# A two-mixer inference step on one core: gated quarters stored from the load queue one slot later, weights of the second mixer in other memory, and its first features interleaved

## The chip, the cores and the metric

The kernel runs on one core of a Trainium2 chip. The time is the device time of one execution in microseconds (us), which for one core is that core's own. Five engines have instruction queues of their own: TensorE (PE, the matmuls, with PEld for the weight loads that run beside them), VectorE (DVE), ScalarE (ACT), GpSimd (POOL) and SyncE (SP, which here only issues transfers). An instruction that waits holds up everything behind it in its queue.

## The reference

A step of a model with two layers over 1024 prompt rows and 128 sample rows of width 1024 (1152 rows, nine tiles of 128), all in float32. Layer A:

```
proj = xn @ w_in                      # 1024 x 6144: u, v, z of 2048 columns each
u, v = gelu(proj[u, v]);  v = layernorm(v)
s = einsum(causal w_s per group of 256 columns, v) + b_s      # mixes rows in chunks of 128
x = x + (u * s * silu(z)) @ w_out     # 2048 x 1024
```

Layer B is an mLSTM: a projection to 4096 columns, a short causal convolution, block-diagonal q, k and v, gates, a matrix memory of four heads in chunks of 64 rows, and an output projection. The eight running streams bring their memories with them and return them. At the end come a last norm and all new states.

## The kernel before, in words

Every matmul in float32 is done as three products in a faster format: each operand is split into a rounded part (hi, a CAST by ACT) and the remainder (lo, a subtraction by DVE, both at L89 and L90 in `split`), and hi·hi, lo·hi and hi·lo are added up in PSUM. A weight tile is therefore ready only when a load has landed, ACT has cast it and DVE has subtracted.

The program runs in stages, in this order.

1. The v projection of layer A (to about 222 us): a loop over four column blocks c and nine row tiles n (L403 on). In the first column block the row tiles are normalised, transposed on PE and split into `Xh` and `Xl` on the way (`norm`, `enter_a`).
2. The u and z projections with the gating, sixteen features f of 128 columns (about 222 to 658 us, L463 to L567). Per feature there are seven products i = 0 to 6, each for two pairs p of row quarters (288 rows each); a product is 12 matmuls of 288 columns. Seven products give the four quarter results of u and z by adding and subtracting the sums (a scheme like Strassen's), so results stay in PSUM or SBUF between products: product 0 leaves `c1` (L497, a copy by ACT out of the accumulator `al`), product 2 goes on in `al` and gives u of the first quarter after a gelu (L503), product 3 leaves `e5`, products 4 and 5 give the two z quarters (add, tanh, multiply, times `Sg`), product 6 gives the other u quarter `y`. Product 2 of a pair cannot start before the copy `c1` of this pair is done, since it writes over `al`.
   `Sg` is the spatial gate: three loads `vh` of v rows, a normalisation by ACT (L531), matmuls `s_` with the group's weights (L539 to L546). Every second feature, `Group` loads and prepares the next group's weights (`wr`, `bs`, `wT`, `rsb`).
   Gated quarters (`uq`, and `y` in the tile `c1`) are written to memory `o_d` by `rows_of` (L481), whose DMA is issued by ACT. The weights of the next features (`fetch_uz`, `prep_uz`) come over SP's queue; two of the seven combinations are sums built by POOL (L369 to L377).
3. The output projection of layer A (658 to 872 us, L638 on), which reads `o_d` back as `or`, splits it into `os`, and adds the residual in `half_out`.
4. Layer B's features (872 to about 1150 us, L811 on), three row blocks b for each feature: the `Feature` class, with `inputs`, then `values` and `keys` one and two steps later. Its first weights are loaded by `w_first` (L664).
5. Gates, decode streams, memory chunks, the output and the last norm (to 1992 us).

PE's instructions are kept in the program's order (class `Ordered`). The order of the other engines and of the queues is set when the program is built, by a scheduler that estimates durations; a tile pool says how many buffers a name has, and where a pool is closed and another opened in its place, the new tiles wait for the last readers of the old ones.

Of the kernel before, what the change touches and what calls it, by code (L numbers as in the profile page):

```python
# [15 lines left out]
P = 128  # L16
# [54 lines left out]
def trunk_kernel(ctx: ExitStack, tc: tile.TileContext, ins: dict, outs: list):  # L71
# [116 lines left out]
    QT = 288  # L188
    KH = KD // 2
    Xh = xp.tile([P, KD, NT * P], F32R, name="Xh")  # L190
    Xl = xp.tile([P, KD, NT * P], F32R, name="Xl")

    S1, S2, S4 = ([xp.tile([P, 2, KH, QT], F32R, name=f"{nm}_{p}") for p in range(2)] for nm in ("S1", "S2", "S4"))
    aw = X_stack.enter_context(tc.tile_pool(name="aw", bufs=1))
# [91 lines left out]
    class Group:  # L286
# [12 lines left out]
        def transposed(self):  # L299
            wT = self.wT = aw.tile([P, 2, P], F32, name="wT")  # L300
            tp = ps.tile([P, P], F32, name="sm")
            T.transpose(tp, self.wr, ident)
            V.tensor_copy(out=wT[:, 0], in_=tp)
            self.w16 = aw.tile([SL, SB, SL], F32, name="w16")
            V.tensor_copy(out=self.w16, in_=wT[:SL, 0, :SL].unsqueeze(1).to_broadcast([SL, SB, SL]))
# [6 lines left out]
        def sums(self):  # L312
            rs = ps.tile([P, 2, P], F32, name="sm")
            T.matmul(rs[:, 0], ones, self.wT[:, 0], start=True, stop=True)
            T.matmul(rs[:, 1], ones, self.wT[:, 1], start=True, stop=True)
            self.rsb = aw.tile([P, 2, P], F32, name="rsb")
            V.tensor_copy(out=self.rsb, in_=rs)
# [64 lines left out]
    for c in range(4):  # L382
        if c:
            wv = [split_b(fetch_b(a_w[:, k, E + c * DH:E + (c + 1) * DH])) for k in range(KD)]
        for n in range(NT):
# [25 lines left out]
            pv = ps.tile([P, DH], F32, name="sm")  # L411
            for k in range(KD):
                mm3(pv, Xh[:, k, ns], Xl[:, k, ns], wv[k][:, 0], wv[k][:, 1], k == 0, k == KD - 1)
            if c == 0 and n == 0:
                enter_a(1)
                xs_[2] = norm(2, V)
                x_[3] = load_x(3)
            vt = vp.tile([P, DH], F32, name="v")
# [41 lines left out]
    def both(s):  # L460
        return s[:, 0], s[:, 1]

    for f in range(NF):  # L463
        g, i2 = divmod(f, 2)
# [16 lines left out]
        def rows_of(o, q):  # L481
            A.dma_start(out=o_d[f * P:(f + 1) * P, quarter(q)], in_=o)

        for i in range(7):
            for p in range(2):
                q0, q1 = 2 * p, 2 * p + 1
# [14 lines left out]
                elif i == 2:  # L501
                    uq[p] = az.tile([P, QT], F32, name="uq", bufs=3)
                    A.activation(out=uq[p], in_=acc, func=AF.Gelu_apprx_tanh)  # L503
                elif i == 3:
                    e5[p] = az.tile([P, QT], F32, name="e5")
                    A.copy(out=e5[p], in_=acc)
                    G.tensor_tensor(out=e5[p], in0=e5[p], in1=c1[p], op=ALU.add)
                elif i in (4, 5):
                    z, q = (e5[p], q1) if i == 4 else (U2[p], q0)
                    V.tensor_tensor(out=z, in0=acc, in1=z, op=ALU.add)  # L510
                    t = az.tile([P, QT], F32, name="t", bufs=3)
                    A.activation(out=t, in_=z, func=AF.Tanh, scale=0.5)
                    V.scalar_tensor_tensor(out=t, in0=t, scalar=1.0, in1=z, op0=ALU.add, op1=ALU.mult)
                    G.tensor_tensor(out=t, in0=t, in1=Sg[:, quarter(q)], op=ALU.mult)
                    if i == 4:
                        tz[p] = t
                    else:
                        V.scalar_tensor_tensor(out=uq[p], in0=uq[p], scalar=0.5, in1=t, op0=ALU.mult, op1=ALU.mult)
                        rows_of(uq[p], q0)
                else:  # L520
                    y = c1[p]
                    V.tensor_tensor(out=y, in0=acc, in1=y, op=ALU.add)
                    A.activation(out=y, in_=y, func=AF.Gelu_apprx_tanh)
                    V.scalar_tensor_tensor(out=y, in0=y, scalar=0.5, in1=tz[p], op0=ALU.mult, op1=ALU.mult)
                    rows_of(y, q1)
            if i < 3:

# [4 lines left out]
                if b == 2:  # L532
# [5 lines left out]
                    S.dma_start(out=sgu_v[0].rearrange("b t e -> (b t) e")[:, f * P:(f + 1) * P], in_=gv[:, 2])  # L538
            if 0 < i < 4:  # L539
                b = i - 1  # L540
                s_ = ps.tile([P, 3, P], F32, name="sm")
# [5 lines left out]
            if i2 == 1 and g + 1 < 8:  # L547
                if i == 3:
                    grp = Group(g + 1)
                elif i > 3:  # L550
                    (grp.transposed, grp.sample, grp.sums)[i - 4]()
            if f + 1 < NF:
# [3 lines left out]
            else:  # L556
# [8 lines left out]
                if i == 6:  # L565
                    split_wo(0, 9)
    X_stack.close()  # L567

# [3 lines left out]
    xs_stack = ExitStack()  # L572
    kp_ = xs_stack.enter_context(tc.tile_pool(name="kp", bufs=1, side="right"))
    ow_stack = ExitStack()
    w2 = ow_stack.enter_context(tc.tile_pool(name="w2", bufs=7))
    ow = ow_stack.enter_context(tc.tile_pool(name="ow", bufs=5))
    xh = [xtp.tile([P, KD, BT], F32R, name="xh") for _ in range(NB)]
# [27 lines left out]

    xa = ow.tile([P, NT, DH], F32, name="xa", bufs=1)
    xs_ = {}

    def half_out(n, c, po):

        cs = slice(c * DH, (c + 1) * DH)
        xv = xa[:, n] if c == 0 else ow.tile([P, DH], F32, name="xb", bufs=3)
        S.dma_start(out=xv, in_=rows(n, ins["x_prompt"], ins["x_sample"])[:, cs])
# [16 lines left out]
    for c in range(2):  # L630
        for b in range(NB):
            po = [ps.tile([P, DH], F32, name="sm") for _ in range(3)]
            for f in range(NF):
# [20 lines left out]
                if c == 1 and b and f in (4, 8, 12):  # L654
                    enter(3 * b - 4 + f // 4)
            for j in range(3):
                half_out(3 * b + j, c, po[j])
    ow_stack.close()
    A_stack.close()
    wp = ctx.enter_context(tc.tile_pool(name="wp", bufs=6))  # L660
    rawp = ctx.enter_context(tc.tile_pool(name="rawp", bufs=4))


    w_first = load_w(b_w[:, :, 0:P])  # L664
    bw_stack = ExitStack()
# [27 lines left out]
    class Feature:  # L693
# [31 lines left out]
        def inputs(self, b):  # L725
# [7 lines left out]
            if b == 2:  # L733
                A.copy(out=xms[:, :, 3:], in_=pm[:, 256:].rearrange("p (b j) -> p b j", b=SB))
                self.xsc = bw.tile([P, P], F32, name="xsc")
                A.copy(out=self.xsc, in_=pm[:, 256:])
            xc = self.xc[b] = bw.tile([P, BT], F32, name="xc", bufs=4)
            parts = [(xc[:, :npr], [xmp[:, b * BT + t:b * BT + t + npr] for t in range(4)])]
# [72 lines left out]
    done = {}  # L811
    feats = [Feature(0)]
    for t in range(3 * NF):
        f, b = divmod(t, NB)
        ft = feats[f]
        ft.inputs(b)
        if b == 0:
            ft.gate_weights()
        if f == 0 and b < 2:
            for n in ((6,), (7, 8))[b]:  # L820
                enter(n)
        if t:
            feats[(t - 1) // NB].values((t - 1) % NB)
        if t > 1:
            feats[(t - 2) // NB].keys((t - 2) % NB)
        if b == 1:
            ft.history()
            if f + 1 < NF:
                feats.append(Feature(f + 1))
            else:  # L830
                z_weights(0)
# [743 lines left out]
```

## Time and profile before

| | |
|---|---|
| runs shown | 1994.90, 2000.48, 2000.66 us; median 2000.48 us |
| profiled execution | 1994.11 us, of it 1992.4 us span from the first to the last instruction |
| mean granted TensorE clock | 0.985 of full speed |
| busy: PE, PEld | 1910.1 us (96%), 1690.7 us (85%) |
| busy: DVE, ACT, POOL | 1261.9 us (63%), 848.2 us (43%), 652.4 us (33%) |
| memory | 203.07 MB read, 123.02 MB written, 164 GB/s over the span |

In the profile a row of a timeline gives a start, a duration, the engine, the line in the kernel, what is written and read, and in brackets how long the engine had been idle before and what ended that. `ACTq` and `SPq` are the instructions with which ACT and SP issue transfers. Idle time is worth most on PE, since PE is busy 96% of the time; the other engines' idle time counts only where PE waits for them.

### The profile page before, as it was taken

How to read it: one execution, taken by the hardware profiler on the slowest of the kernel's cores; microseconds unless marked ns; L12 is line 12 of the kernel's file. 1: busy time of each engine (PE TensorE's matmuls, PEld its weight loads, DVE VectorE, ACT ScalarE, POOL GpSimd, SP SyncE). 2: the span in 40 equal slices, each digit the busy share in tenths (PEclk: the TensorE clock that was granted, in tenths of full speed). 3: DMA queues.
4: the chain of work that ended last, by engine and by line, in shares of the span. 5: the costliest groups of instructions: out<-in, count | busy, mean ns of one | idle time of the engine just before them, and what ended most of it. 6: DMA issues, size and time to landing. Idle time of an engine off the chain costs nothing.

```text
span 1992.4 us, 32048 instructions
## 1 busy us (share of the span) xinstructions
PE 1910.1 (96%) x11553; PEld 1690.7 (85%) x11553; DVE 1261.9 (63%) x2490; ACT 848.2 (43%) x1729; POOL 652.4 (33%) x669
## 2 busy tenths in 40 slices
PE   7999999999999899989999999999999999999998
PEld 5888898999999778869999989888977778778887
DVE  4732466666666454556676665222398799799897
ACT  5422444444444333445555554321254344344454
POOL 2000245444444000014444421100045345436466
PEclk9999999999999999999999999999999999999999
DMA  6222332233333745415555564777898788786433
GB/s 210 85 95 76 106 89 84 86 98 100 97 92 103 228 151 155 152 57 143 161 154 164 163 181 141 212 227 251 256 314 271 243 282 258 242 261 200 152 122 127
DMA packets 345692, 328.22 MB, mean 165 GB/s; under 512 B 28165, under 2 KB 276949, under 8 KB 345533
## 3 DMA queue, kind: packets, MB, share of 16 engines
q1 hardware_dynamic: 279596, 251.59, 41.6%
q10 hardware_dynamic: 65936, 74.58, 11.8%
q8 instruction: 91, 1.49, 0.3%
q14 instruction: 69, 0.56, 0.1%
HBM read 203.07 MB, written 123.02 MB: 164 GB/s over the span
## 4 chain that ended last, share of the span: by engine, by line
PE 45%; DVE 12%; DMA 9%; ACT 2%; issue 2%; POOL 1%; SPq 1%; ACTq 0%; POOLq 0%; DVEq 0%
PE sm L58 45%; DVE Cst L1265 2%; DMA cw<-cw_d 2%; DVE c L1116 2%; DMA raw<-in_b_w_in 1%; DVE Cl L90 1%; DVE qT L1239 1%; DMA out<-c 1%; DMA c<-in_state_mlstm_C 1%; DMA st_d<-w 1%; DVE raw L1348 1%; DVE bst L1305 1%; DMA vv<-vb_d 1%; DVE x L1367 1%; DMA raw<-in_b_w_out 1%
## 5 line engine op out<-in xcount | busy, mean ns | idle before, releaser
L58 PE MATMUL sm<-xh,w 128*128 128x384 f32 x1536 | 414.9, 344 | 8.5 <-issue 6.9
L58 PEld LDWEIGHTS sm<-xh,w 128*128 128x128 f32 x1536 | 285.1, 191 | 17.0 <-issue 13.3
L58 PE MATMUL sm<-xl,w 128*128 128x384 f32 x768 | 262.8, 342 | 1.2 <-DVE xl L90 1.2
L58 PE MATMUL sm<-Xh,w 128*128 128x288 f32 x1024 | 222.5, 302 | 18.8 <-ACT c L497 18.8
L90 DVE TENSOR_TENSOR w<-r,w 128x512 fp32r<-128x512 f32 x176 | 140.3, 806 | 117.3 <-ACT w L89 117.1
L58 PE MATMUL sm<-w,o 128*128 128x512 f32 x864 | 209.8, 398 | 2.6 <-ACT o L89 1.2
L58 PE MATMUL sm<-w,os 128*128 128x512 f32 x864 | 200.2, 393 | 6.7 <-ACT os L89 6.7
L58 PEld LDWEIGHTS sm<-w,os 128*128 128x128 f32 x864 | 162.6, 189 | 42.7 <-ACT os L89 9.2
L58 PEld LDWEIGHTS sm<-w,o 128*128 128x128 f32 x864 | 159.8, 188 | 40.6 <-ACT hn L1317 1.7
L58 PEld LDWEIGHTS sm<-Xh,w 128*128 128x128 f32 x1024 | 169.8, 190 | 22.5 <-ACT c L497 21.5
L58 PE MATMUL sm<-w,Xh 128*128 128x512 f32 x576 | 182.4, 398 | 4.3 <-ACT Xh L89 2.9
L58 PE MATMUL sm<-S,w 128*128 128x288 f32 x1152 | 165.6, 300 | 0.0
L90 DVE TENSOR_TENSOR w<-raw,w 128x1024 fp32r<-128x1024 f32 x44 | 56.8, 1290 | 168.9 <-ACT w L89 164.0
L58 PEld LDWEIGHTS sm<-S,w 128*128 128x128 f32 x1152 | 158.2, 191 | 0.0
L58 PE MATMUL sm<-Xl,w 128*128 128x288 f32 x512 | 152.1, 297 | 0.0
L58 PEld LDWEIGHTS sm<-xl,w 128*128 128x128 f32 x768 | 146.7, 191 | 1.4 <-DVE xl L90 1.4
L89 ACT CAST w<-r 128x512 fp32r<-128x512 f32 x176 | 105.8, 618 | 70.5 <-POOL r L371 34.6
L58 PEld LDWEIGHTS sm<-w,Xh 128*128 128x128 f32 x576 | 109.4, 192 | 28.6 <-ACT Xh L89 3.5
L58 PE MATMUL sm<-w,Xl 128*128 128x512 f32 x288 | 113.7, 395 | 0.0
L89 ACT CAST w<-raw 128x1024 fp32r<-128x1024 f32 (+1 forms) x56 | 55.2, 988 | 129.9 <-DMA raw<-in_b_w_in 105.4
L90 DVE TENSOR_TENSOR os<-or,os 128x384 fp32r<-128x384 f32 x96 | 53.0, 556 | 89.3 <-ACT os L89 89.3
L58 PE MATMUL sm<-va,k 128*128 128x258 f32 (+1 forms) x768 | 103.8, 284 | 4.5 <-ACT ev L1109 1.7
(306 smaller groups left out, 3745.9 us busy)
## 6 DMA issues: line engine op xcount, KB each, us to landing
c<-in_state_mlstm_C SPq DMA_DIRECT2D x64, 512.0 KB
out<-c SPq DMA_DIRECT2D x64, 512.0 KB
r<-in_a_w_in SPq DMA_DIRECT2D x96, 256.0 KB
or<-o_d SPq DMA_DIRECT2D x96, 192.0 KB
raw<-in_b_w_in SPq DMA_DIRECT2D x32, 512.0 KB
qT<-q_d SPq DMA_DIRECT2D x40, 256.0 KB
vh<-v_d SPq DMA_DIRECT2D x48, 192.0 KB
vb_d<-st ACTq DMA_DIRECT2D x48, 192.0 KB
```

What stands on the lines that cost most here:

```text
L58: ins = fn(*args, **kw)
L89: first = A.copy(out=hi, in_=src)
L90: (lo_eng or V).tensor_tensor(out=lo, in0=src, in1=f32(hi), op=ALU.subtract)
L1116: V.scalar_tensor_tensor(out=c0[:, cc], in0=c0[:, cc], scalar=decB[:, d.h, 8 + b:9 + b], in1=pc, op0=ALU.mult, op1=ALU.add)
L1239: V.tensor_tensor(out=u.g["qT"], in0=u.g["qT"], in1=u.g["cw"][:, 1:2].to_broadcast([P, DC, P]), op=ALU.mult)
L1265: V.scalar_tensor_tensor(out=Cst[:, c, a, :w], in0=Cst[:, c, a, :w], scalar=decB[:, h, n:n + 1], in1=pc, op0=ALU.mult, op1=ALU.add)
L1305: V.bn_stats(out=bst[:, a], in_=hn[:, a, :256])
L1348: V.scalar_tensor_tensor(out=og[:, c], in0=u.pT[:, c], scalar=colB[:, HNG, 4 * h + c:4 * h + c + 1], in1=g["sk"][:, c], op0=ALU.mult, op1= ...
L1367: V.tensor_tensor(out=xv, in0=xv, in1=py, op=ALU.add)
```

## The change

Eight things are changed.

- `rows_of` no longer issues a store at once from ACT. It puts it on a list, and the list is issued from SP's queue at the end of the next product slot (the last feature's at the end of the stage).
- Of the two multiplications by `Sg` per pair, that of product 5 moves from POOL to DVE; that of product 4 stays on POOL but is written in the slot of product 5.
- The gate's matmuls `s_` for the three row blocks stand after products 2, 3 and 4 instead of 1, 2 and 3.
- `Group` for the next group starts at product 0 instead of 3, its parts at products 2, 4 and 6 instead of 4, 5 and 6; `wT` and `rsb` have two buffers.
- In the v projection, the second row tile's transposes stand inside the first tile's loop, at k = 5.
- `S1` and `S2` change places in memory, and lie before `Xh` and `Xl`; the output projection's pools are ordered anew, and the row tiles `xa` and `xb` have a pool of their own.
- The pools of layer B's weights are opened, and `w_first` loaded, before the last row block's `half_out`, instead of after all of them.
- Layer B's first two features take turns: (feature, block) = (0,0), (0,1), (1,0), (1,1), (0,2), (1,2), then as before; the last row tiles (6, 7, 8) are transposed during (1,0) and (1,1) instead of (0,0) and (0,1); `xc` has six buffers.

```diff
@@ layer A's features
         def rows_of(o, q):
-            A.dma_start(out=o_d[f * P:(f + 1) * P, quarter(q)], in_=o)
+            late.append(lambda f=f: S.dma_start(out=o_d[f * P:(f + 1) * P, quarter(q)], in_=o))
 
         for i in range(7):
+            rows_out_, late = late, []
...
-                    G.tensor_tensor(out=t, in0=t, in1=Sg[:, quarter(q)], op=ALU.mult)
                     if i == 4:
                         tz[p] = t
                     else:
+                        V.tensor_tensor(out=t, in0=t, in1=Sg[:, quarter(q)], op=ALU.mult)
+                        G.tensor_tensor(out=tz[p], in0=tz[p], in1=Sg[:, quarter(q1)], op=ALU.mult)
...
+            for fn in rows_out_:
+                fn()
...
-            if 0 < i < 4:
-                b = i - 1
+            if 1 < i < 5:
+                b = i - 2
...
-                if i == 3:
-                    grp = Group(g + 1)
-                elif i > 3:
-                    (grp.transposed, grp.sample, grp.sums)[i - 4]()
+                if i == 0:
+                    nxt_grp = Group(g + 1)
+                elif i % 2 == 0:
+                    (nxt_grp.transposed, nxt_grp.sample, nxt_grp.sums)[i // 2 - 1]()
@@ the first row tiles
             for k in range(KD):
+                if c == 0 and n == 0 and k == 5:
+                    enter_a(1)
+                    xs_[2] = norm(2, V)
+                    x_[3] = load_x(3)
                 mm3(pv, Xh[:, k, ns], Xl[:, k, ns], wv[k][:, 0], wv[k][:, 1], k == 0, k == KD - 1)
-            if c == 0 and n == 0:
-                enter_a(1)
-                xs_[2] = norm(2, V)
-                x_[3] = load_x(3)
@@ the end of layer A's output projection
+            if c == 1 and b == 2:
+                ow_stack.close()
+                A_stack.close()
+                rawp = ctx.enter_context(tc.tile_pool(name="rawp", bufs=4))
+                wp = ctx.enter_context(tc.tile_pool(name="wp", bufs=6))
+                w_first = load_w(b_w[:, :, 0:P])
             for j in range(3):
                 half_out(3 * b + j, c, po[j])
-    ow_stack.close()
-    A_stack.close()
-    wp = ctx.enter_context(tc.tile_pool(name="wp", bufs=6))
-    rawp = ctx.enter_context(tc.tile_pool(name="rawp", bufs=4))
-    w_first = load_w(b_w[:, :, 0:P])
@@ layer B's features
-    feats = [Feature(0)]
-    for t in range(3 * NF):
-        f, b = divmod(t, NB)
+    feats = [Feature(0), Feature(1)]
+    steps = [(0, 0), (0, 1), (1, 0), (1, 1), (0, 2), (1, 2)] + [divmod(t, NB) for t in range(2 * NB, NF * NB)]
+    for t, (f, b) in enumerate(steps):
```

How the instructions stand on three queues. First ACT's, at the end of one feature of stage 2 and the start of the next; `c1_3276` and `c1_3291` are the two finished quarters `y` of the feature that ends, `c1_3594` and `c1_3609` the copies that the next feature's product 2 waits for. Before:

```order
L482 DMA o_d_89<-c1_3276 128x288
L523 ACTIVATE c1_3291<-c1_3291 128x288
L497 COPY c1_3594<-sm_3581 128x288
L482 DMA o_d_89<-uq_3356 128x288
L482 DMA o_d_89<-c1_3291 128x288
L497 COPY c1_3609<-sm_3596 128x288
L89 CAST w_3747<-r_3390 128x512
L482 DMA o_d_89<-uq_3370 128x288
```

The same place of the changed kernel (`c1_3274` and `c1_3289` end, `c1_3592` and `c1_3607` are the copies):

```order
L526 ACTIVATE c1_3274<-c1_3274 128x288
L89 CAST w_3699<-r_3527 128x512
L526 ACTIVATE c1_3289<-c1_3289 128x288
L499 COPY c1_3592<-sm_3579 128x288
L499 COPY c1_3607<-sm_3594 128x288
L89 CAST w_3742<-r_3397 128x512
L89 CAST w_3784<-r_3439 128x512
```

The second copy stood behind two stores, and now follows the first one directly.

SP's queue at the same place, where loads of weights `r` and of gate rows `vh` stand (`out_2` is a store of the sample rows' v, `gv` and `wr` are small loads for it and for the next group). Before:

```order
L538 DMA out_2<-gv_3693 128x128
L535 DMA gv_3991<-in_a_ln_g 128x128
L535 DMA gv_3991<-in_a_ln_b 128x128
L291 DMA wr_4045<-in_a_w_s 128x128
L204 DMA r_3708<-in_a_w_in 128x4x128
L204 DMA r_3750<-in_a_w_in 128x4x128
L475 DMA vh_3874<-v_d1_91 128x3x128
L204 DMA r_3789<-in_a_w_in 128x4x128
```

The changed kernel, with the four stores of the feature that ends:

```order
L483 DMA o_d_89<-uq_3357 128x288
L483 DMA o_d_89<-c1_3274 128x288
L483 DMA o_d_89<-c1_3289 128x288
L204 DMA r_3703<-in_a_w_in 128x4x128
L483 DMA o_d_89<-uq_3371 128x288
L204 DMA r_3745<-in_a_w_in 128x4x128
L204 DMA r_3787<-in_a_w_in 128x4x128
L476 DMA vh_3872<-v_d1_91 128x3x128
```

One store stands between the first and the second weight load, the other three ahead of both.

ACT's queue where layer A ends and layer B begins: `xb` are the last row tiles, `w_8426` and `w_8387` the first weight tile of layer B. Before:

```order
L615 DMA x1_d6_125<-xb_8372 128x512
L621 ACTIVATE xs_8376,ss2_8377<-xb_8372 128x512
L615 DMA x1_d7_126<-xb_8386 128x512
L621 ACTIVATE xs_8390,ss2_8391<-xb_8386 128x512
L615 DMA x1_d8_127<-xb_8400 128x512
L621 ACTIVATE xs_8404,ss2_8405<-xb_8400 128x512
L89 CAST w_8426<-raw_8424 128x1024
L89 CAST w_8595<-raw_8593 128x1024
```

The changed kernel:

```order
L626 DMA x1_d6_125<-xb_8390 128x512
L632 ACTIVATE xs_8394,ss2_8395<-xb_8390 128x512
L89 CAST w_8387<-raw_8385 128x1024
L626 DMA x1_d7_126<-xb_8404 128x512
L632 ACTIVATE xs_8408,ss2_8409<-xb_8404 128x512
L89 CAST w_8468<-raw_8466 128x1024
L626 DMA x1_d8_127<-xb_8418 128x512
L632 ACTIVATE xs_8422,ss2_8423<-xb_8418 128x512
```

The first cast moved ahead of two row tiles' work, the second ahead of one's.

## Rows read from the trace of the kernel before

**Rows 1.** The page, busy time of each engine.

```profile
PE   1910.1 (96%) x11553; PEld 1690.7 (85%) x11553; DVE 1261.9 (63%) x2490; ACT 848.2 (43%) x1729; POOL 652.4 (33%) x669
```

**Rows 2.** Waits of PE, whole run: total us, times, longest.

```profile
PE sm L58 <- ACT c L497: 18.8, 11, 2.5
...
PE sm L58 <- DVE w L305: 3.3, 5, 0.9
...
PE sm L58 <- ACT vh L531: 2.5, 1, 2.5
```

**Rows 3.** Busy us by window: PE, PEld, DVE, ACT, POOL, clock, DMA.

```profile
220.00:600.00 380.00, 356.31 (x2613) 350.36 (x2612) 246.55 (x420) 166.25 (x398) 180.09 (x171) 0.98 0.34 97
```

**Rows 4.** Timeline of all engines over one feature's end: start, us, work, idle before.

```profile
466.62 1.27 ACT L531 ACTIVATE vh<-vh,nmr,rstd 128x128 f32<-128x128 f32 x3 [2.15 <-DMA vh<-v_d]
...
469.87 0.23 DVE L296 COPY bs<-bs 128x128 f32<-128x128 f32 x1 [2.75 <-DMA bs<-in_a_b_s]
...
475.49 0.63 ACT L89 CAST w<-r 128x512 fp32r<-128x512 f32 x1 [0.75 <-POOL r L371]
...
477.21 0.38 ACT L497 COPY c<-sm 128x288 f32<-128x288 f32 x1
...
477.39 0.83 PE L58 MATMUL sm<-wT,vh 128*128 128x128 f32 x6
...
478.81 1.38 POOL L377 TENSOR_TENSOR r<-r 128x512 f32<-128x512 f32 x1 [0.68 <-POOL t L514]
478.97 1.53 DVE L518 SCALAR_TENSOR_TENSOR uq<-uq,t 128x288 f32<-128x288 f32 x1
...
481.39 0.45 DVE L518 SCALAR_TENSOR_TENSOR uq<-uq,t 128x288 f32<-128x288 f32 x1
481.50 0.33 ACTq L482 DMA_DIRECT2D o_d<-c  x1
481.87 0.40 ACT L497 COPY c<-sm 128x288 f32<-128x288 f32 x1 [4.28 <-DVE uq L518]
...
482.32 0.40 PE L58 MATMUL sm<-Xh,w 128*128 128x288 f32 x1 [2.52 <-ACT c L497]
...
485.31 4.28 PE L58 MATMUL sm<-S,w 128*128 128x288 f32 x24
```

**Rows 5.** Timeline of PE, one product of a feature without a wait.

```profile
504.01 3.35 PE L58 MATMUL sm<-S,w 128*128 128x288 f32 x24
```

**Rows 6.** Timeline of SP and PE where stage 2 ends and 3 begins.

```profile
658.04 0.33 SPq L198 DMA_DIRECT2D gB<-in_norm_g  x1
658.42 1.37 SPq L645 DMA_DIRECT2D or<-o_d  x3
...
664.69 3.67 PE L58 MATMUL sm<-w,os 128*128 128x512 f32 x8 [6.68 <-ACT os L89]
```

**Rows 7.** Timeline where stage 3 ends and layer B begins.

```profile
871.69 0.38 SPq L144 DMA_DIRECT2D raw<-in_b_w_in  x1
...
874.03 0.75 DVE L627 SCALAR_TENSOR_TENSOR xs<-xb,rr,gB 128x512 f32<-128x512 f32 x1
...
877.36 1.04 ACT L89 CAST w<-raw 128x1024 fp32r<-128x1024 f32 x1 [3.61 <-DMA raw<-in_b_w_in]
...
878.44 1.22 DVE L90 TENSOR_TENSOR w<-raw,w 128x1024 fp32r<-128x1024 f32 x1 [1.34 <-ACT w L89]
...
879.72 1.01 PE L58 MATMUL sm<-xh,w 128*128 128x384 f32 x2 [0.23 <-DVE w L90]
...
894.56 0.44 PE L58 MATMUL sm<-xh,w 128*128 128x384 f32 x1 [1.45 <-ACT xh L89]
896.15 0.45 PE L58 MATMUL sm<-xl,w 128*128 128x384 f32 x1 [1.15 <-DVE xl L90]
```

**Rows 8.** Timeline of PE in the head, between the first two row tiles.

```profile
19.07 1.91 PE L58 MATMUL sm<-ident,xs 128*128 128x128 f32 x16
23.87 1.22 PE L58 MATMUL sm<-w,Xh 128*128 128x512 f32 x2 [2.89 <-ACT Xh L89]
```

More of the change, by code (lines that the diff above doesn't have):

```diff
@@ L189, in trunk_kernel @@
     KH = KD // 2
+    S2, S1, S4 = ([xp.tile([P, 2, KH, QT], F32R, name=f"{nm}_{p}") for p in range(2)] for nm in ("S2", "S1", "S4"))
     Xh = xp.tile([P, KD, NT * P], F32R, name="Xh")
     Xl = xp.tile([P, KD, NT * P], F32R, name="Xl")
-    S1, S2, S4 = ([xp.tile([P, 2, KH, QT], F32R, name=f"{nm}_{p}") for p in range(2)] for nm in ("S1", "S2", "S4"))
     aw = X_stack.enter_context(tc.tile_pool(name="aw", bufs=1))
@@ L299, in transposed @@
         def transposed(self):
-            wT = self.wT = aw.tile([P, 2, P], F32, name="wT")
+            wT = self.wT = aw.tile([P, 2, P], F32, name="wT", bufs=2)
             tp = ps.tile([P, P], F32, name="sm")
@@ L315, in sums @@
             T.matmul(rs[:, 1], ones, self.wT[:, 1], start=True, stop=True)
-            self.rsb = aw.tile([P, 2, P], F32, name="rsb")
+            self.rsb = aw.tile([P, 2, P], F32, name="rsb", bufs=2)
             V.tensor_copy(out=self.rsb, in_=rs)
@@ L461, in both @@
         return s[:, 0], s[:, 1]
+    late = []
     for f in range(NF):
@@ L566, in trunk_kernel @@
                     split_wo(0, 9)
+        if i2 == 1 and g + 1 < 8:
+            grp = nxt_grp
+    for fn in late:
+        fn()
     X_stack.close()
@@ L573, in trunk_kernel @@
     kp_ = xs_stack.enter_context(tc.tile_pool(name="kp", bufs=1, side="right"))
+    xa_stack = ExitStack()
+    xap = xa_stack.enter_context(tc.tile_pool(name="xap", bufs=1, side="right"))
     ow_stack = ExitStack()
+    ow = ow_stack.enter_context(tc.tile_pool(name="ow", bufs=5))
     w2 = ow_stack.enter_context(tc.tile_pool(name="w2", bufs=7))
-    ow = ow_stack.enter_context(tc.tile_pool(name="ow", bufs=5))
     xh = [xtp.tile([P, KD, BT], F32R, name="xh") for _ in range(NB)]
@@ L604, in enter @@
         transpose_x(xs_.pop(n), lambda ks: (xh[b][:, ks, js], xl[b][:, ks, js]))
-    xa = ow.tile([P, NT, DH], F32, name="xa", bufs=1)
+    xa = xap.tile([P, NT, DH], F32, name="xa")
     xs_ = {}
@@ L611, in half_out @@
         cs = slice(c * DH, (c + 1) * DH)
-        xv = xa[:, n] if c == 0 else ow.tile([P, DH], F32, name="xb", bufs=3)
+        xv = xa[:, n] if c == 0 else xap.tile([P, DH], F32, name="xb", bufs=3)
         S.dma_start(out=xv, in_=rows(n, ins["x_prompt"], ins["x_sample"])[:, cs])
@@ L655, in trunk_kernel @@
                     enter(3 * b - 4 + f // 4)
+            if c == 1 and b == 2:
[4 more added lines that the diff above has]
+                w_first = load_w(b_w[:, :, 0:P])
             for j in range(3):
                 half_out(3 * b + j, c, po[j])
-    ow_stack.close()
-    A_stack.close()
-    wp = ctx.enter_context(tc.tile_pool(name="wp", bufs=6))
-    rawp = ctx.enter_context(tc.tile_pool(name="rawp", bufs=4))
-    w_first = load_w(b_w[:, :, 0:P])
+    xa_stack.close()
     bw_stack = ExitStack()
@@ L736, in inputs @@
                 A.copy(out=self.xsc, in_=pm[:, 256:])
-            xc = self.xc[b] = bw.tile([P, BT], F32, name="xc", bufs=4)
+            xc = self.xc[b] = bw.tile([P, BT], F32, name="xc", bufs=6)
             parts = [(xc[:, :npr], [xmp[:, b * BT + t:b * BT + t + npr] for t in range(4)])]
@@ L818, in trunk_kernel @@
             ft.gate_weights()
-        if f == 0 and b < 2:
+        if (f, b) in ((1, 0), (1, 1)):
             for n in ((6,), (7, 8))[b]:
                 enter(n)
[L822 to L825, printed above, removed]
+        for j, part in ((t - 1, Feature.values), (t - 2, Feature.keys)):
+            if j >= 0:
+                part(feats[steps[j][0]], steps[j][1])
         if b == 1:
             ft.history()
-            if f + 1 < NF:
-                feats.append(Feature(f + 1))
+        if t == 4 or (f > 1 and b == 1):
+            if len(feats) < NF:
+                feats.append(Feature(len(feats)))
             else:
```

## The prediction

> **What bounds the kernel now.** First the page's busy times: PE is busy 1910 of 1992 us, no other engine over 63% [rows 1]. So the kernel is bound by PE, and a change that adds and removes no matmul, as this one, can win only PE's idle time and the time in which PE runs at a lower clock. Then PE's waits, to see whose fault the idle time is: 18.8 us, the largest entry, are eleven waits for one ACT instruction, the copy c at L497 [rows 2]. Then the windows, to see where: in the stage of u and z (220 to 600) PE is idle 380 - 356.3 = 23.7 us, and the mean granted clock is 0.98 [rows 3]: for a part of the stage PE runs at the lower of its two levels, 1.2 instead of 2.4 GHz. Last the timeline of one such wait. The reader is to see a queue there: ACT is idle 4.28 us before the copy, and it isn't the copy's own input that is late, but the stores ahead of it. The store of c is issued at 481.50, the copy runs right behind at 481.87, and PE starts at 482.32 after 2.52 us idle [rows 4]. The stores wait for DVE, DVE for POOL.
>
> **The change, part by part.**
>
> *Stores from ACT to SP (the largest part).* The first copy ran at 477.21 (0.38 us). With nothing between them the second runs directly behind it, to about 477.97, instead of 481.87 + 0.40: 4.3 us earlier, against a wait of 2.5 [rows 4]. So all eleven waits should go, 18.8 us. What is late next? The product after the copy also moves: the six gate matmuls that stood ahead of it (477.39, 0.58 us until the next product at 477.97) come after it now, so it would start at 477.39 [rows 4]. ACT's order moves one gelu (about 0.43) ahead of the first copy. If ACT's weight cast at 475.49 still waits for POOL (L371) at the same time, the first copy ends at 477.21 + 0.43 + 0.38 = 478.0, which is 0.6 us late. I expect the cast to be earlier, because two things that made it late go: ACT's wait of 2.15 us for a vh load at 466.62, and DVE's 2.75 us for a load of bs at 469.87 [rows 4]; vh is now normalised about a feature ahead, and the group starts three products earlier. With 2 us gained there the copies are over 1 us early. I leave 1 us for the whole stage; the bounds are 0 and 0.6 x 16 = 10.
>
> *Gate matmuls one slot later, group earlier.* The wait for vh, 2.5 us, was the first feature's; one slot (over 3.3 us, the length of a product [rows 5]) covers it. The five waits for w at L305, 3.3 us [rows 2], are group steps in neighbouring slots; now a free slot lies between. Both go.
>
> *The clock that comes back.* After the gap at 482.32, 24 matmuls took 4.28 us, against 3.35 in a feature without a wait [rows 4, 5]: a gap costs more than itself. For the stage I take 2% of 380 us = 7.6 [rows 3] (0.975 and 0.985 would round to it, so 5.7 to 9.5). It comes back only if the gaps go.
>
> *One multiplication per pair from POOL to DVE.* 32 more on DVE. The nearest row is uq at L518, the same size: 0.45 us alone, 1.53 when it starts just after POOL's r at 478.81 [rows 4]. So 14 to 49 us more on DVE, which is busy 247 of 380 us here [rows 3]: it stays below 80%. PE waits for DVE only two products later, which hides it; I cost it at nothing. Here a rule speaks against the change. The Trainium skill ("SBUF — State Buffer", section "Who interferes with whom") says that a DVE instruction with two inputs in SBUF and a GpSimd instruction that reads SBUF exclude each other, and the second one fully blocks. The trace agrees: uq started 0.16 us after POOL's r and ended 0.31 us after it. By that rule the upper end holds for many of the 32; it would turn into time only by the first rival below.
>
> A second page bears on the stores. The Trainium skill ("DMA: Bandwidth & Descriptors", section "Issuing engines are not separate DMA queues") says that spreading transfers over issuing engines saves only the time to issue them, "which is usually small". By it alone the move is worth 0.33 us of ACT's time per store and nothing on PE, and the sum below would lose 26 us. The trace shows what that leaves out: a 0.33 us issue with 4.28 us of waiting behind it.
>
> *Where stage 2 ends.* The load gB is issued at 658.04, the first or loads at 658.42, and PE starts at 664.69 after 6.68 idle [rows 6]. The changed order puts one store (0.33 us, and about 150 KB of traffic) between gB and or; nothing else there is earlier. Cost 0.8; bounds -1 and 1.5.
>
> *Where layer B begins.* The load raw is issued at 871.69, as the last matmul ends; ACT casts at 877.36, DVE subtracts from 878.44 to 879.66, and the third matmul, the first that needs DVE's part, runs at 879.72 [rows 7]. Now the load needs only memory that PE leaves six features of the loop earlier (54 matmuls; eight took 3.67 us at a lowered clock [rows 6], so even at twice that speed 12 us), and from issue to cast it took 5.7: it has landed. The cast still waits for PE's end and for one store and one Square on ACT: it ends near 873.1. DVE does its part behind the first half of xs, which ends where the row 874.03 begins, so until 875.25, and the third matmul runs at 875.3: 4.4 us gained. The waits at 894.56 and 896.15 (1.45 + 1.15) are for the last row tiles, transposed just before they are used [rows 7]. In the new order ACT has its copies and casts of the two first steps behind it by then, and about 1.9 us of other matmuls stand between: 2.6 gained. Together 7.0; bounds 3 and 9 (a slower clock that goes with the second gap).
>
> *Head.* Sixteen transposes at 19.07, then 2.89 us of waiting [rows 8]. Eight of them now stand in the first tile's loop, and the casts for the second tile run ahead of a table load. But half of Xl stands on DVE behind a copy that waits for a load until 20.15 us, so the second tile starts near 20.4 instead of 23.87. Gain 3.5; bounds 0 and 5.
>
> *Other memory, six xc buffers, pools.* No transfer or instruction more; nothing.
>
> *Sum.* Stage 2: 18.8 + 2.5 + 3.3 + 7.6 - 1.0 = 31.2. Head 3.5, stage end -0.8, layer B 7.0: 40.9 us. The profiled execution took 1994.11, so its like would take 1953.2. The runs shown lie 0.8, 6.4 and 6.6 us above the profiled one, 4.6 in the mean; I forecast 1957.8, rounded to 1958. Behind 1150 us the order of all engines is the same but for a few transfers, so nothing is counted.
>
> **Rivals.**
>
> 1. *The wait moves to the first copy.* ACT still waits for POOL's weight sum (L371) ahead of both copies. For it: the 0.75 us at 475.49 [rows 4]. The rule of the page on SBUF in the Trainium skill, cited above, speaks for it too, since POOL gets more two-input neighbours on DVE. Against: the chain ahead of it loses 2 us and more. Price: 0.6 us in each of 16 features and half of the clock's 7.6: 13.4, less the 1 already counted, about 1970. Chance 0.15.
>
> 2. *The transitions bring nothing.* Head and layer B stay bound by loads or by DVE: 10.5 us less, 1968. Chance 0.07.
>
> 3. *SP's queue is held up, and the kernel is slower.* The store of the second uq waits for DVE, which finished it at 481.84 [rows 4]; behind it on SP stand the next weight loads and then the vh loads, and ACT does vh ahead of the copies. The wait of 2.15 us for vh at 466.62 shows that ACT really stops for such a load. By the order, the copies have about 4 us to spare; if vh comes later than that, every feature waits for the excess. At 4 + 31/16 = 6 us the stage's gain is gone, from 6.6 us on the kernel is slower. At 8 us: 16 x 4 = 64, so 1958 + 64 = 2022. Against: vh is loaded a feature ahead, and the stores of y wait only for the product's own end. Chance 0.05.
>
> 4. *It doesn't do what it says:* the copies were never behind the stores alone; ACT reaches them as late, because gelu and casts wait for DVE that is busier. 1999. Against: the first copy, behind the same gelu, was in time. Chance 0.03.
>
> **How the numbers follow.** My forecast has 0.70. A measurement of this kernel can tell about 0.3%, 6 us. The lower end: 1 for the residual, 1.9 for the clock, 1.8 at the stage's end, 2 in layer B, 1.5 in the head, and a run close to the profiled one, not all at once: 1946. The upper end takes in rivals 2 and 1 with some of the medians above: 1975. Outside are rivals 3 and 4, part of 1, and little below. Faster by over 0.3% is the forecast and rivals 1 and 2, 0.92; within it 0.03; slower 0.05.
>
> **What would show it.** In the changed profile PE's waits should no longer name the copy c, w at L305 or vh; in 220 to 600 PE should be busy all but 2 us, at clock 1.00; stage 2 should end near 658 - 31 - 3.5 = 623. ACT's casts should have their waits for POOL, if any, ahead of a copy that is in time. PE's gap between stages 2 and 3 should be 7 to 8 us, that ahead of layer B about 1.5 + 2, and the pair of waits 23 us into layer B gone. Wrong would be: PE waiting for c or for a gate's vh in most features (rivals 1 and 3), SP idle for DVE's uq with loads late behind it, or the stage as long as before with PE at full clock.

## The result, and the profile after

The change makes the kernel faster: 1969.53 us (median of 4 runs, 1961.52 to 1975.91) against 1997.69 us of the kernel before, run on the same chip (4 runs, 1994.72 to 2000.66). The ratio is 0.986, with a 95% interval of 0.981 to 0.990: 28 us. The forecast was 1958, with a range of 1946 to 1975: the direction is right, the time lies in the range, and some 12 us of the forecast gain are missing. The first rival's time, about 1970, is met by chance: its wait, for the copy c in most features, isn't there, as the rows below show. The profiled execution took 1961.52 us, with a span of 1959.8 us against 1992.4.

PE's busy time on the page of the changed kernel, beside [rows 1]:

```profile
PE 1900.5 (97%) x11553; PEld 1681.2 (86%) x11553; DVE 1270.3 (65%) x2522; ACT 850.0 (43%) x1727; POOL 621.4 (32%) x637
```

As many matmuls in 9.6 us less busy time: so much came from a higher clock, on balance, and the rest of the 32.6 us of span from idle time. PE's waits over the whole run (total us, times, longest), beside [rows 2]:

```profile
...
PE sm L58 <- DVE rA L887: 7.5, 1, 7.5
PE sm L58 <- ACT os L89: 6.6, 1, 6.6
PE sm L58 <- ACT c L499: 4.6, 2, 4.2
...
PE sm L58 <- ACT xh L89: 1.2, 1, 1.2
...
PE sm L58 <- DVE xl L90: 1.1, 1, 1.1
```

The waits for w at L305 and for vh are gone, and of eleven waits for the copy c two are left. But one entry is new and large: rA, 7.5 us in one piece. The windows (busy us of PE, PEld, DVE, ACT, POOL, then clock) show what each means:

```profile
220.00:600.00 380.00, 375.43 (x2845) 373.18 (x2844) 273.93 (x490) 184.44 (x432) 162.29 (x159) 1.00 0.36 104
...
1150.00:1170.00 20.00, 15.43 (x44) 3.80 (x45) 6.06 (x18) 0.38 (x1) 0.00 (x0) 0.50 0.54 174
```

In stage 2 PE is busy all but 4.6 of 380 us at clock 1.00, against 23.7 us of idle time at 0.98 [rows 3]. Over the whole stage, 433.4 us before and 403.7 after, PE's idle time falls from 24.6 to 4.6 us and its busy time, for the same matmuls, from 408.8 to 399.1: 20.0 us of waits and 9.7 us of clock. At 1150 it is idle, and then runs at 1.2 GHz, half its clock. Where rA is made and used, in time order:

```profile
1147.26 0.48 ACT L796 COPY qk<-sm 128x384 f32<-128x384 f32 x1
...
1148.45 0.61 ACTq L798 DMA_DIRECT2D k_d<-qk  x1
...
1153.97 1.71 DVE L887 COPY rA<-sm 8x384 f32<-8x384 f32 x3 [11.75 <-DMA c<-in_state_mlstm_C]
...
1154.57 1.44 PE L58 MATMUL sm<-rA,ident 8*4 8x384 f32 x2 [7.55 <-DVE rA L887]
...
1171.02 0.69 PE L58 MATMUL sm<-xh,w 128*128 128x384 f32 x1
```

DVE stands still for 11.75 us before a copy of a few values. PE then does the six rounds of gate matmuls in 1171.02 - 1154.57 = 16.45 us. In the kernel before there was no wait of PE here, and the same rounds ran at full clock:

```profile
1188.71 1.71 DVE L874 COPY rA<-sm 8x384 f32<-8x384 f32 x3 [4.20 <-DMA k_d<-qk]
...
1189.31 0.80 PE L58 MATMUL sm<-rA,ident 8*4 8x384 f32 x2
...
1198.20 0.45 PE L58 MATMUL sm<-xh,w 128*128 128x384 f32 x1
```

That is 8.89 us. The new wait and the low clock behind it cost 7.55 + 7.56 = 15.1 us. Up to it the changed kernel was 42.3 us ahead (the last four matmuls before these rounds start at 1146.16, before at 1188.45); 27.2 us are left behind it, and the later stages end 32.6 us ahead.

At stage 2's end and at layer B's start, beside [rows 6] and [rows 7], one row per step:

```profile
622.84 0.33 SPq L198 DMA_DIRECT2D gB<-in_norm_g  x1
...
623.69 0.90 SPq L656 DMA_DIRECT2D or<-o_d  x2
...
629.41 40.84 PE L58 MATMUL sm<-w,os 128*128 128x512 f32 x170 [6.61 <-ACT os L89]
...
837.20 1.03 ACT L89 CAST w<-raw 128x1024 fp32r<-128x1024 f32 x1
838.33 0.41 PE L58 MATMUL sm<-xh,w 128*128 128x384 f32 x1 [1.53 <-issue]
839.18 1.22 DVE L90 TENSOR_TENSOR w<-raw,w 128x1024 fp32r<-128x1024 f32 x1
840.45 0.63 PE L58 MATMUL sm<-xh,w 128*128 128x384 f32 x2 [1.53 <-DVE w L90]
...
865.45 0.44 PE L58 MATMUL sm<-xh,w 128*128 128x384 f32 x1 [1.23 <-ACT xh L89]
866.95 0.45 PE L58 MATMUL sm<-xl,w 128*128 128x384 f32 x1 [1.06 <-DVE xl L90]
```

The gap between the stages is as long as before. Layer B starts without waiting for a load: its third matmul, the first that needs DVE's part, runs at 840.45 for 879.72, 39.3 us ahead, and the stage before it began 35.3 us ahead (629.41 for 664.69), so 4.0 us are gained here. The pair of waits behind it has stayed.

### The profile page after: what moved, and what is told of

Same layout as the page of the kernel before. It is cut to its first block, busy times and chain, and to the rows that moved or that the text cites. A ratio compares the mean times of both kernels' runs of the same rounds, so it can differ in the third digit from the quotient of the medians.

```text
span 1959.8 us, 32037 instructions
## 1 busy us (share of the span) xinstructions
PE 1900.5 (97%) x11553; PEld 1681.2 (86%) x11553; DVE 1270.3 (65%) x2522; ACT 850.0 (43%) x1727; POOL 621.4 (32%) x637
## 4 chain that ended last, share of the span: by engine, by line
PE 74%; DVE 13%; DMA 7%; ACT 2%; issue 2%; POOL 1%; SPq 1%; ACTq 0%; POOLq 0%; DVEq 0%
PE sm L58 74%; DVE Cst L1278 2%; DMA cw<-cw_d 2%; DVE c L1129 2%; DVE Cl L90 1%; DVE qT L1252 1%; DMA out<-c 1%; DVE raw L1361 1%; DVE bst L1318 1%; DMA c<-in_state_mlstm_C 1%; DMA vv<-vb_d 1%; DMA r<-in_a_w_in 0%; DVE dn L1324 0%; DVE x L1380 0%; DMA st_d<-w 0%
## 5 line engine op out<-in xcount | busy, mean ns | idle before, releaser
L58 PE MATMUL sm<-Xh,w 128*128 128x288 f32 x1024 | 216.3, 298 | 4.6 <-ACT c L499 4.6
L90 DVE TENSOR_TENSOR w<-r,w 128x512 fp32r<-128x512 f32 x176 | 136.1, 779 | 50.3 <-ACT w L89 49.8
```

The source lines that it names most:

```text
L58: ins = fn(*args, **kw)
L90: (lo_eng or V).tensor_tensor(out=lo, in0=src, in1=f32(hi), op=ALU.subtract)
```

## The experiments

Two questions: what the wait for rA is, and which of the edits in stage 2 brought its gain.

**e1: rA in other memory.** Theory: `rA` now takes over memory in which the last `qk` tile lies. In the memory map of a partition that tile lies at bytes 119456 to 122528 before and at 121504 to 124576 after, and rA at 122592 to 127200; so in the changed kernel the copy into rA has to wait until ACT's last stores out of `qk` have landed, not for a state load, as the row's releaser says. In the program as built the copy waits, among earlier stores, for the two out of this tile, and for no state load. (Before, it was the last `qk` tile but one that lay there; the copy waited 4.20 us for its store, as the row above shows, early enough for PE.)

```
+    for nm in ("rF", "rE"):
+        gt.tile([8, NTK], F32, name=nm)      # two unused tiles ahead of gsb: rA lies above qk
```

> The changed kernel with the gate tile rA placed 9 KB higher, above the last qk tile of layer B; nothing else moves. Theory: the two added xc buffers (2 x 1536 bytes) pushed the last qk tile under rA, so that DVE's copy to rA waits for qk's last store; moved away, PE's wait of 7.5 us for rA and the gate matmuls at half the clock behind it (16.4 us from the first to the last pair instead of 8.9) go, some 15 us: a profile near 1947, a median near 1955. Rival: the gates wait for memory traffic (the state loads start earlier now), whatever tile they write; then a wait of about the same size stays and the time stays within 3 us of the changed kernel's.

Measured: 1956.43 us (4 runs, 1953.51 to 1959.78), 0.978 of the kernel before (0.976 to 0.981). The window 900 to 1250 of e1, then DVE's copy in its timeline:

```profile
900.00:1250.00 350.00, 346.68 (x2056) 320.70 (x2055) 211.41 (x460) 185.61 (x377) 118.01 (x164) 0.99 0.58 168
```

```profile
1145.08 1.70 DVE L889 COPY rA<-sm 8x384 f32<-8x384 f32 x3
```

The copy has no wait in brackets, and PE is busy 346.7 us at clock 0.99; in the changed kernel it is 339.9 at 0.96.

The theory held: 13 us by the medians (15 if each is set against the kernel before of its own runs). The state load is still there, so it was not the cause.

**e2: six buffers for xc in the kernel before.** The cause by itself: this one number moves the tiles behind xc.

```
-            xc = self.xc[b] = bw.tile([P, BT], F32, name="xc", bufs=4)
+            xc = self.xc[b] = bw.tile([P, BT], F32, name="xc", bufs=6)
```

> The kernel before with one number changed: six xc buffers instead of four. Theory: qk moves up by 3072 bytes here too, DVE's copy to rA waits for the last qk store, PE waits some 7 us and then runs its gate matmuls at half the clock: 10 to 16 us slower than before, near 2010. Rival (a buffer count that nobody waits for costs nothing, as the prediction had it): within 3 us of before.

Measured: 2013.23 us, ratio 1.006 (1.004 to 1.009). The wait and the slow rounds appear in a kernel that is otherwise the one before:

```profile
1197.86 1.44 PE L58 MATMUL sm<-rA,ident 8*4 8x384 f32 x2 [7.74 <-DVE rA L874]
```

A buffer count that adds no instruction costs 14 us.

**e3: the stores alone.** The kernel before, with `rows_of` through SP one slot later and nothing else.

```
-            A.dma_start(out=o_d[...], in_=o)
+            late.append(lambda f=f: S.dma_start(out=o_d[...], in_=o))
```

> The kernel before with the gated quarters' stores alone moved to SP's queue, one product slot later. Theory: the eleven waits for the copy c at L497 (18.8 us) go with the stores, and with them most of the stage's lost clock (7.6): 20 to 26 us faster than before, about 1975; the waits for L305 (3.3) and the first vh (2.5) stay. Rival: the first copy then waits for POOL's weight sum (L371) and DVE, since their chain is as late as before; half of it, 9 to 13 us, about 1987.

Measured: 2008.77 us, ratio 1.005 (1.004 to 1.007): slower. PE's, ACT's and SP's waits in the stage (total us, times, longest):

```profile
PE sm L58 <- DVE w L305: 14.8, 7, 2.9
PE sm L58 <- ACT e L508: 13.5, 8, 3.1
PE sm L58 <- DVE e L512: 3.1, 4, 0.8
PE sm L58 <- ACT vh L535: 2.4, 1, 2.4
PE sm L58 <- ACT c L499: 0.9, 2, 0.7
...
ACT vh L535 <- DMA vh<-v_d: 126.8, 28, 9.6
...
SPq L483 <- DVE c L526: 98.1, 30, 8.2
SPq L483 <- DVE uq L520: 70.7, 20, 8.0
```

The waits for c go from 18.8 to 0.9 us, as the prediction's largest term says, but the others rise from 5.8 to 33.8. SP now stands up to 8 us at a store that waits for DVE; the vh loads behind it come late, ACT waits for them 127 us in all (71.0 before, longest 3.7), and copies and additions behind vh are late for PE. That is the mechanism of the third rival; neither the theory nor the rival of this run's own forecast had it. The Trainium skill ("DMA: Bandwidth & Descriptors", section "Issuing engines are not separate DMA queues") holds that spreading transfers over issuing engines saves only issue time. The trace here shows a cost that this doesn't count: which queue holds a waiting store decided what else was late, in this run for 9 us.

**e4: the change with the stores on ACT.** The reverse edit.

> The changed kernel with the stores issued at once from ACT again; all its other edits stay. Theory: ACT's second copy stands behind a store that waits for DVE again, so 10 to 20 us of waits for the copy c come back and with them clock: 15 to 25 us slower than the changed kernel. Rival: the other edits of the stage (gate rows a feature ahead, group earlier, one product on DVE) bring the chain ahead of the stores early enough; at most 5 us slower, waits for c under 5 us.

Measured: 1974.67 us in one run. PE's waits for c in the stage:

```profile
PE sm L58 <- ACT c L499: 6.0, 4, 4.3
```

This kernel still has the wait for rA (7.97 us), so it is to be set against the changed kernel's 1969.53: 5 us slower, and 4.3 of the 6.0 us are one wait that the changed kernel has too (4.2). The theory (10 to 20 us of waits) fell; the rival's bound on the waits, 5 us, is passed by 1.0, and that on the time by less than a single run can tell. So with the other edits in place the copies are mostly in time even behind the stores: the stores alone were not what held them.

**e5, e6, e7: one edit undone each.** All on e1.

```
e5:  -  V.tensor_tensor(out=t, in0=t, in1=Sg[:, quarter(q)], op=ALU.mult)
     +  G.tensor_tensor(out=t, in0=t, in1=Sg[:, quarter(q)], op=ALU.mult)
e6:  -  if 1 < i < 5: b = i - 2          # gate matmuls
     +  if 0 < i < 4: b = i - 1
e7:  -  if i == 0: nxt_grp = Group(g + 1);  parts at i = 2, 4, 6
     +  if i == 3: nxt_grp = Group(g + 1);  parts at i = 4, 5, 6
```

> The changed kernel with rA in other memory (as e1), and of the change's edits in stage 2 one undone: the 32 multiplications t*Sg are on POOL again, not on DVE. E4 has shown that PE's waits for the copy c go even with the stores on ACT's queue, so another edit of this stage does it. Theory A: it is this one, since POOL, which also makes the differences of the weights (L371 to L377) that ACT's casts wait for, has less queued ahead of them; then the waits for c, w or e come back, 8 us or more in 220 to 600, and PE's busy time there falls from about 374 to 366 or less. Theory B: the multiplications are hidden on either engine, and the later gates or the earlier group do it; then under 3 us of waits come back.

> As e1, with another single edit undone: the six gate matmuls of a feature stand in the slots 1 to 3 again, one product after the vh they use is normalised. Theory B1: this was the gate of the queue; PE waits for vh or for c come back, 8 us or more in 220 to 600. Theory A (POOL is relieved by the multiplications): only the first feature's wait for vh returns, 2 to 3 us, and the stage is otherwise as in e1.

> As e1, with a third single edit undone: the group's load and its three steps stand in the slots 3 to 6 again. By my prediction the five waits for w at L305 come back with it, 3.3 us, and DVE's stop for the load of bs, with a wait for c in every second feature: 5 to 15 us less PE time in 220 to 600. The rival: the steps alone cost 3.3 us and nothing else follows.

Measured, one run each: e5 1945.14, e6 1968.72, e7 1969.10 us. PE's waits in the stage, first of e6, then of e7:

```profile
PE sm L58 <- ACT c L499: 9.8, 6, 2.0
PE sm L58 <- ACT vh L536: 2.9, 1, 2.9
```

```profile
PE sm L58 <- DVE w L305: 10.4, 7, 2.3
PE sm L58 <- ACT c L499: 5.5, 2, 4.5
```

Theory A falls: with the multiplications on POOL no wait comes back. The gates' slot and the group's slots each hold some 12 us: with either undone, the stage takes 416 to 417 us for 404. In e7 the waits for w are most of it, 10.4 us where the prediction had 3.3; the wait for c in every second feature that e7's forecast had isn't there (the 4.5 is the one that e1 has too, with 4.2). In e6 the waits have come back as B1 said, and ACT's queue shows why. Before, and in e6, three normalisations of vh stand in it ahead of the first tanh of product 4, in nearly every feature; with the gates a slot later, only two. The third is the row of [rows 4] at 466.62, with 2.15 us of waiting for its load; the tanh runs right behind it, and at the same place of e11 (below) ahead of it. First the tanh before, then both of e11:

```profile
467.79 0.43 ACT L512 ACTIVATE t<-e 128x288 f32<-128x288 f32 x1
```

```profile
446.82 0.43 ACT L512 ACTIVATE t<-e 128x288 f32<-128x288 f32 x1
...
449.71 0.49 ACT L532 ACTIVATE vh<-vh,nmr,rstd 128x128 f32<-128x128 f32 x1 [1.60 <-DMA vh<-v_d]
```

ACT still waits for the load, but with the tanh done. On the average of fourteen features the tanh starts 22.4 us after its feature's first product before and 22.5 in e6, but 19.1 in e11, 18.8 in e7 and 19.0 in e1: the multiplications behind it, and the stores behind those, can start over 3 us earlier.

**e11: these two alone, in the kernel before.** Stores on ACT, multiplications on POOL.

> The kernel before with two of the change's edits of stage 2 alone: gate matmuls one slot later and the group's load and steps in the slots 0, 2, 4 and 6, with two buffers each for wT and rsb. All stores stay on ACT at once, all multiplications by Sg on POOL (those of the second and fourth quarter one slot later, since the gates they read come later). Theory B, after e4 to e7 (stage 2 from its first product to its last: before 433.4 us, the change 403.7, with the gates undone 416.1, with the group undone 417.0, with the stores undone 407.8, with the multiplications on POOL 398.5): the two edits alone bring the stage to 400 to 410, PE's waits for c there to under 6, and the time to about 1971, 0.986 of the kernel before. Rival, my prediction's first term: the copies c stand behind stores that wait for POOL and DVE, so with the stores on ACT at least half of the 18.8 us stay: the stage takes 415 or more, and the time is 1980 or more.

Measured: 1973.14 us, ratio 0.988 (0.985 to 0.990). PE's waits in the stage:

```profile
PE sm L58 <- ACT c L497: 8.9, 8, 2.8
```

The time is within 2 us of what theory B gave, and under the rival's 1980; the waits are 8.9 instead of under 6. Two edits that the prediction had priced at 5.8 us bring most of what the whole change brings in this stage.

The length of stage 2, from the start of its first product to the start of its last matmul, in each profile:

| kernel | stage 2, us |
|---|---|
| before; e2 (the same code here) | 433.4; 436.8 |
| stores alone (e3) | 447.7 |
| gates and group alone (e11) | 409.7 |
| gates, group, stores (e5; again; e10 below) | 398.5; 398.8; 400.3 |
| gates, group, multiplications (e4) | 407.8 |
| all (after; e1; e9 below) | 403.7; 403.7; 404.4 |
| all but the gates (e6); all but the group (e7) | 416.1; 417.0 |

Read by means: 435.1 to 409.7 by gates and group (25.4), to 399.2 by the stores (10.5), and back to 403.9 by the multiplications (4.7 lost). The parts depend on each other: the stores alone lose 12.6, and where the multiplications are on DVE already (e4) they bring 3.9, which is hardly more than the 3.4 between two profiles of the same code in the first line.

**e5 again, timed.**

> The kernel of e5 again (the change, rA moved, t*Sg on POOL), now timed, since one run gave 1945.1 against 1953.5 to 1959.8 in e1. If a multiplication on DVE beside POOL's work costs time, as the stage's 398.5 against 403.7 us says, its ratio to the kernel before is 0.975 or lower, below e1's 0.978; if the one run was a lucky one, it is 0.978 again.

Measured: 1956.35 us (4 runs, 1950.56 to 1961.45), ratio 0.979 (0.976 to 0.982), the same as e1. The stage is again 5 us shorter and the time is not: from the gate rounds to the end this run took 808 us, the first run of the same kernel 798, e1 802. The last stages scatter by more than the gain, and whether it reaches the end is not settled. Of the 5 us, 3.2 are PE's idle time (4.6 to 1.4 us) and the rest its clock, and nearly all of the idle time is one wait, in the second feature. In the changed kernel:

```profile
248.67 1.52 POOL L371 TENSOR_TENSOR r<-r 128x512 f32<-128x512 f32 x1
249.06 1.43 DVE L519 TENSOR_TENSOR t<-t,Sg 128x288 f32<-128x288 f32 x1
250.14 1.48 POOL L375 TENSOR_TENSOR r<-r 128x512 f32<-128x512 f32 x1
250.53 1.40 DVE L521 SCALAR_TENSOR_TENSOR uq<-uq,t 128x288 f32<-128x288 f32 x1
251.85 0.44 DVE L525 TENSOR_TENSOR c<-sm,c 128x288 f32<-128x288 f32 x1
251.96 0.44 ACT L514 ACTIVATE t<-U 128x288 f32<-128x288 f32 x1 [3.91 <-DVE uq L521]
...
254.09 0.68 ACT L499 COPY c<-sm 128x288 f32<-128x288 f32 x2
...
254.52 0.40 PE L58 MATMUL sm<-Xh,w 128*128 128x288 f32 x1 [4.16 <-ACT c L499]
```

Without the multiplication on DVE (e5 again):

```profile
248.79 0.44 DVE L525 TENSOR_TENSOR c<-sm,c 128x288 f32<-128x288 f32 x1
...
251.78 0.68 ACT L499 COPY c<-sm 128x288 f32<-128x288 f32 x2
...
252.21 0.40 PE L58 MATMUL sm<-Xh,w 128*128 128x288 f32 x1 [1.44 <-ACT c L499]
```

Two DVE instructions of 0.45 us end 0.3 us after POOL's sums, after 1.43 and 1.40 us; the addition behind them is 3.1 us later, and ACT's copy 2.3. This is the rule that the prediction cited from the Trainium skill ("SBUF — State Buffer", section "Who interferes with whom"), and the trace agrees; it now reached PE.

**e9: the two gaps that were left.** gB is loaded later, the pool of `or` waits for its memory tile by tile, and the last row tiles enter a step earlier.

```
-    ow = ...tile_pool(name="ow", bufs=5)
+    ow = ...tile_pool(name="ow", bufs=5, reuse_waits="tile")
-    gB = load_gB(ins["norm_g"][1], kp_, "gB")             # ahead of the loop
+                if c == 0 and b == 0 and f == 4:          # inside it
+                    gB = load_gB(ins["norm_g"][1], kp_, "gB")
-        if (f, b) in ((1, 0), (1, 1)): enter 6, then 7 and 8
+        if t in (1, 2): enter 6, then 7 and 8
```

> As e1, with two more edits at the two gaps that the change left. First, the load of gB is issued inside the output projection, and the pool of the or tiles waits tile by tile for the memory that it takes over, so that the first or load waits for the last product that reads S2, not for the stage's last matmul: by my reading PE's gap of 7.0 us between the stages falls to 2 to 4. A rival says that the gap is the load's own latency behind SP's stores, and it stays over 5. Second, the last three row tiles of layer B are transposed one step earlier: the pair of waits (1.2 + 1.1 us) at its second row tile goes. Together 5 us below e1, about 1951; against the kernel before about 0.975.

Measured: 1953.47 us, ratio 0.978 (0.975 to 0.980). SP and PE where the stage ends:

```profile
622.29 0.38 SPq L483 DMA_DIRECT2D o_d<-uq  x1
622.77 0.39 SPq L656 DMA_DIRECT2D or<-o_d  x1
...
627.11 0.73 PE L58 MATMUL sm<-w,os 128*128 128x512 f32 x2 [3.53 <-ACT os L89]
628.74 0.79 PE L58 MATMUL sm<-w,os 128*128 128x512 f32 x1 [0.90 <-DVE os L90]
```

The gap falls from 7.0 to 3.5 + 0.9 us, since the first `or` load no longer stands behind gB and the stage's last matmul (which of the two counts for how much was not tried). The pair of waits in layer B, 2.3 us, is gone. That is 4.9 us in the trace and 3 in the medians, within the intervals.

**e10: both.** E9 with the multiplications on POOL.

> E9 (rA in other memory, or loads waiting tile by tile, gB later, last row tiles a step earlier) with t*Sg on POOL as in e5. If the parts add up: stage 2 at 398 to 399 us, PE's gap behind it 3 to 4, no pair of waits in layer B, and 5 us below e9's 1953.5: about 1948, 0.974 of the kernel before. If DVE's relief and the gaps share a cause (in e5 the pair of waits in layer B was gone already), 3 us.

Measured: 1948.36 us (5 runs, 1941.80 to 1953.08), ratio 0.974 (0.972 to 0.977). It is the lowest median of all, 21 us below the changed kernel; 13 of that are certain, the memory of rA, and the rest is no larger than the intervals of e1, e9 and e10. That the pair of waits in layer B was missing in the first run of e5 already is no second cause: there PE ran the products ahead of it at a clock of 0.72 (834 to 846 us) and came late itself.

## Why the prediction was right and wrong

- *"Stage 2: 31.2 us."* The sum holds (29.7 between the two profiles, 31.2 between the means of the table), its working does not. With nothing between them the second copy does run directly behind the first, and the waits for c do go with the stores (e3). The failing step is to count these 18.8 us as gained by that edit, with 1 us left for what is late next: alone it lengthened the stage by 12.6 us, and on top of gates and group it brought 10.5, or 3.9. The row with 4.28 us of idle time ahead of the copy [rows 4] named the wait that ended last, and taking it away alone showed the next ones. The prediction asked what is late next only for the copy, not for the loads behind the stores on their new queue; the third rival did, and gave it 0.05.
- *"Gate matmuls one slot later, group earlier: 2.5 + 3.3."* Priced by the waits that PE showed for them by name. Measured 25.4 together. Their effect is on the queues, but the prediction's reason for it, that ACT's stop for vh and DVE's for bs go, holds only in part: in e11 ACT still waits 58.3 us for vh in the stage (71.0 before) and DVE 16.0 for bs (16.9). What changed for the gates is what stands behind such a stop: one normalisation less ahead of the tanh, which comes over 3 us earlier. For the group it is PE's own waits for w, 10.4 us when it is late (e7). That these two make up the 25.4 between them is argued from e6, e7 and e11; neither edit was tried alone in the kernel before.
- *"One multiplication per pair from POOL to DVE: nothing."* It cost 4.7 us of the stage, by the mechanism whose upper end the prediction worked out and then held to be hidden; whether the whole time is longer by it isn't shown (e5 again).
- *"The clock comes back if the gaps go, 7.6."* Seen: 0.98 to 1.00, and 9.7 us less busy time for the same matmuls.
- *"Head 3.5."* Mostly not there. PE's 2.89 us for Xh [rows 8] were that one execution's: three other profiles with the same code in the head show 1.52, 0.72 and 0.44 us, and start stage 2 at 220.2 to 220.4 us, not at 224.3. The changed kernels start it at 218.9 to 221.9, in the middle one 219.1. So some 1 us is shown, not 3.5; the 5.5 between the two profiles are mostly bad luck of the profile before.
- *"Stage end -0.8."* The gap is 6.6 for 6.7 us: nothing, which lies within its bounds of -1 and 1.5.
- *"Layer B 4.4 + 2.6."* The start gained 4.0. The second gap stayed at 2.3 for 2.6: ACT's casts were still behind the convolution, and ACT waited 1.64 us for DVE's steps of it at 861.82. With the row tiles a step earlier it went (e9).
- *"Other memory, six xc buffers, pools: nothing. Behind 1150 us nothing is counted."* This is the term that made the forecast miss. It cost 13 us (e1), 14 alone (e2). The prediction counted instructions and transfers; what changed was whose memory a tile takes over. The order of the engines stayed, the time at which a wait ends did not.

Set against e1, in which that one assumption is true, the forecast sum of 40.9 us stands beside a measured 43. That agreement is luck in good part: gates and group brought 20 us more than their term, and the stores with their share of the clock some 15 less. And the 1969.53 lies in the range because the range was wide enough for 13 us that no term of it stood for.

## What to carry to other kernels

A wait that names a store ahead of a copy tells what ended last, not what to remove: before moving a waiting instruction to another queue, list what will stand behind it there, and look on the way that leads to the wait for instructions that stop for something not yet needed (here the third vh ahead of the tanh). A buffer count or the order of pools is an edit like any other: compare the memory map, and for each tile on PE's path ask which transfer last uses its place. And a gap that one profile shows is worth what several profiles of it show.

## What the runs showed of the hardware that was not expected

After 7.5 us without work PE ran the gate rounds at a granted clock of 0.50 of full speed (1.2 GHz), 16.4 us for 8.9: the slow stretch cost as much again as the wait. In e2 it was the same (7.7 us, then 1.44 us for a row that takes 0.80). The last 800 us of the program, untouched by the edits, took 798 and 808 us in two profiles of one kernel, a difference larger than any term of the sum but the first.
